# Gate matmuls of a recurrent unit on halves of the array's rows

## The chip, the cores and the metric

The kernel runs on one core of one Trainium2 chip. The metric is the device time of one launch in microseconds, as the median of several runs. The core's engines work side by side and wait for each other by semaphores: the matrix engine (PE, with its weight loads listed as PEld), the vector engine (DVE), the scalar engine (ACT), GpSimd (POOL), and SyncE (SP), which here issues most of the transfers.

## The reference

A decoder block: one wide input projection, dilated attention as one branch, a gated linear recurrence (RG-LRU) as the other, a merge, an output projection and a layer norm. There are 2048 positions of 1024 features. The change lies in the recurrence's gates, which are block-diagonal: 16 blocks of 64 features, each with a 64x64 matrix for either gate.

```python
def rg_lru(x, w_r, b_r, w_i, b_i, lam):
    xb = x.reshape(B, S, LRU_BLOCKS, LRU_BLOCK_WIDTH)      # 16 blocks of 64
    r = sigmoid(einsum('bsgi,gij->bsgj', xb, w_r).reshape(B, S, C) + b_r)
    i = sigmoid(einsum('bsgi,gij->bsgj', xb, w_i).reshape(B, S, C) + b_i)
    log_a = -LRU_C * r * softplus(-lam)
    a = exp(log_a)
    u = sqrt(maximum(-expm1(2.0 * log_a), 0.0)) * (i * x)
    # h_t = a_t h_{t-1} + u_t along the positions
```

## The kernel before

Everything is held with features on the 128 partitions and positions along the row, in four chunks (`c`, 0 to 3) of 512 positions. A feature tile has 128 features, so it holds two gate blocks. The numbers are float32; a product of two is made of three matmuls, high by high, high by low and low by high part, each part rounded to the engine's one-pass float32 (`F32R`).

The kernel has three stages, of which the first, up to about 1420 us, makes the input projection. Its loop (line 881) goes over `T` ticks: in each, `product` (line 597) issues 12 matmuls of 128x512 into one of four PSUM banks (`q`, line 614), then the events of that tick are issued (`prep_w`, line 268: rounding the next weights on ACT at line 274 and their low part on DVE or POOL), then `run_chains`, and then `evacuate`, by which DVE or ACT reads the bank. Half way through the 12 matmuls `run(pe_late)` (line 617) issues small PE work that was put off: transposes of values (`vtp`, line 366) and the gates of the recurrence (`g`, lines 482 to 484).

All else is done by generators, the chains. Each `yield Ask(...)` is a point where a chain goes on in a later tick: when enough ticks have passed (`lag`), enough of the 32 shared buffers are free (`need`, `keep`), its condition holds, and the tick's allowance of engine time (`LEN`, 2.75 us, less the estimates that `Ask` names) isn't used up. The estimates decide the order of the instructions on every engine; they are fixed numbers in the code.

`lru(i, c, ub)` (line 437) is the chain of feature tile `i` and chunk `c`: 8 tiles by 4 chunks are 32 of them. In order: at 16 of the 32 it brings both gates' weights to `gr` (lines 448 and 449, on SP's queue), already laid out on the host as 128x128 with two 64x64 blocks on the diagonal and zeros beside them. It makes the convolution `v`; splits the weights into `gw`, high and low part of either gate, four matrices of 128 columns (lines 466 and 467); splits `v` into `vh` and `vl`; and puts off `gates()` to the middle of the next tick's matmuls. `gates()` makes one bank for each gate, three matmuls each. Two ticks later ACT takes the tanh of either bank (lines 495 and 496; a sigmoid is made of a tanh), with the biases `brh`, then an exp and two more functions; DVE multiplies `ti` by `v` (line 500), and the rest ends in a scan (line 517). `gate["busy"]` keeps a second chain from issuing its gates before the tanh of the first are issued; the two banks of tag `g` are all that there are.

`lo_` and `up_` (line 301) are the partitions 0 to 63 and 64 to 127.

Of the kernel before, what the change touches and what calls it, by code (L numbers as in the profile page):

```python
# [8 lines left out]
F32 = mybir.dt.float32  # L9
F32R = mybir.dt.float32r  # L10
AF = mybir.ActivationFunctionType
ALU = mybir.AluOpType
# [3 lines left out]
P = 128  # L16
# [4 lines left out]
CH = 512  # L21
# [10 lines left out]
def hybrid_block_kernel(ctx: ExitStack, tc: tile.TileContext, a: dict, out: bass.AP):  # L32
    nc = tc.nc
    sp, act, dve, pool, pe = nc.sync, nc.scalar, nc.vector, nc.gpsimd, nc.tensor

    def flat(t):
        return t.bitcast(F32)
# [37 lines left out]
    brh = cst.tile([P, 2, 8], F32, name="brh")  # L75
# [33 lines left out]
    def pe_later(lag, fn):  # L109
        pe_late.append((now["n"] + lag, fn))  # L110
# [27 lines left out]
    ps = stA.enter_context(tc.tile_pool(name="ps", bufs=2, space=PSUM))  # L138
# [5 lines left out]
    def take(name, dt=F32R):  # L144
        if not vacant:
            raise RuntimeError(f"no slot at {now['n']}: {[x[1].name if hasattr(x[1],'name') else x[1] for x in home.values()]} chains {len(chains)}")
        i = vacant.pop(0)
        t = sl_p.tile([P, CH], dt, tag=f"s{i}", name=name)
        home[id(t)] = (i, t)
        return t  # L150

    def give(*ts):
        for t in ts:
            vacant.append(home.pop(id(t))[0])

    def give_sent(*ts):

        for t in ts:
            later(2, lambda t=t: give(t))
# [69 lines left out]
    def tt(eng, out, in0, in1, op):  # L229
        eng.tensor_tensor(out=out, in0=in0, in1=in1, op=op)  # L230
# [70 lines left out]
    lo_, up_ = slice(0, 64), slice(64, P)  # L301
# [129 lines left out]
    GLG, GW = {}, {}  # L431
# [5 lines left out]
    def lru(i, c, ub):  # L437
        nm = f"{i}_{c}"
        f = FT_U + i
        if c == 1 and i in put_off:  # L440
            yield Ask(lag=0, need=1, keep=1, cond=lambda: len(ub_free) > 1)
            ub = ub_free.pop(0)
            sp.dma_start(ub[:, 3:3 + CH], u_scr[i])
        bring_gw = c in ((0, 1) if i in put_off else (0, 2))
        if bring_gw:
            yield Ask(lag=0, need=1, keep=1)
            gr = take("gr" + nm, F32)
            sp.dma_start(gr[:, 0:P], a["wr"][i])
            sp.dma_start(gr[:, P:2 * P], a["wi"][i])
        if c == 1 and i in put_off:  # L450
            yield Ask(lag=4)
        yield Ask(lag=0, need=1, keep=6, cond=lambda: gate["live"] < 2 and begun[i] == c, ACT=1.3, DVE=2.7)
        gate["live"] += 1
        begun[i] += 1
        v = take("v" + nm, F32)
        act.activation(ub[:, 0:3], ubs[:, i, c, 0:3], AF.Copy)
        act.activation(v, ub[:, 0:CH], AF.Identity, scale=lrn[:, 0, i:i + 1], bias=lr[:, 4, i:i + 1])
        for j in range(1, 4):
            dve.scalar_tensor_tensor(out=v, in0=ub[:, j:j + CH], scalar=lrn[:, j, i:i + 1], in1=v,
                                     op0=ALU.mult, op1=ALU.add)  # L460
        act.activation(ubs[:, i, c + 1, 0:3], ub[:, CH:CH + 3], AF.Copy)
        ub_free.append(ub)
        if bring_gw:
            yield Ask(ACT=.4, DVE=.4, lag=2, need=1, keep=1)
            w = GW[i] = take("gw" + nm)
            act.activation(w[:, 0:2 * P], gr[:, 0:2 * P], AF.Copy)
            tt(dve, w[:, 2 * P:], gr[:, 0:2 * P], flat(w[:, 0:2 * P]), ALU.subtract)
            give(gr)
        yield Ask(lag=0, cond=lambda: gated[i] == c)
        gw = GW[i].rearrange("p (l j f) -> p l j f", l=2, j=2)  # L470
        yield Ask(need=2, keep=1, ACT=.66, DVE=.75)
        vh, vl = take("vh" + nm), take("vl" + nm)
        act.activation(vh, v, AF.Copy)
        tt(dve, vl, v, flat(vh), ALU.subtract)
        yield Ask(lag=2, cond=lambda: not gate["busy"])
        gate["busy"] = True
        pg = []

        def gates():
            for j in range(2):  # L480
                g = ps.tile([P, CH], F32, tag="g", name=f"g{j}{nm}", bufs=2)
                pe.matmul(g, gw[:, 0, j], vh, start=True, stop=False)
                pe.matmul(g, gw[:, 0, j], vl, start=False, stop=False)  # L483
                pe.matmul(g, gw[:, 1, j], vh, start=False, stop=True)
                pg.append(g)
            give(vh, vl)
            if c in ((0, 3) if i in put_off else (1, 3)):
                give(GW[i])

        pe_later(1, gates)  # L490
        gated[i] = c + 1
        yield Ask(lag=2, need=3, keep=1, ACT=3.3, DVE=.75)
        gate["busy"] = False
        tr, ti, e = take("tr" + nm, F32), take("ti" + nm, F32), take("e" + nm, F32)
        act.activation(tr, pg[0], AF.Tanh, scale=0.5, bias=brh[:, 0, i:i + 1])
        act.activation(ti, pg[1], AF.Tanh, scale=0.5, bias=brh[:, 1, i:i + 1])
        act.activation(e, tr, AF.Exp, scale=sp2n[:, i:i + 1], bias=sp2n[:, i:i + 1])
        act.activation(e, e, AF.Identity, scale=0.5, bias=half_t)
        act.activation(tr, tr, AF.Tanh, scale=sp2[:, i:i + 1], bias=sp2[:, i:i + 1])
        dve.scalar_tensor_tensor(out=ti, in0=ti, scalar=1.0, in1=v, op0=ALU.add, op1=ALU.mult)  # L500
        give(v)
        yield Ask(need=2, keep=1, ACT=2.0, DVE=2.2)
        s, w = take("sq" + nm, F32), take("nw" + nm, F32)
        act.activation(s, tr, AF.Sqrt)

        dve.scalar_tensor_tensor(out=w, in0=tr, scalar=1.0, in1=e, op0=ALU.add, op1=ALU.mult)
        dve.scalar_tensor_tensor(out=e, in0=w, scalar=2.0, in1=e, op0=ALU.subtract, op1=ALU.mult)
        dve.scalar_tensor_tensor(out=tr, in0=tr, scalar=2.0, in1=e, op0=ALU.mult, op1=ALU.mult)
        give(w)
        yield Ask(ACT=.66, DVE=1.5)  # L510
        act.activation(tr, tr, AF.Identity, bias=one_t)
        dve.scalar_tensor_tensor(out=s, in0=s, scalar=-1.0, in1=e, op0=ALU.mult, op1=ALU.mult)
        tt(dve, s, s, ti, ALU.mult)
        give(e, ti)
        yield Ask(need=1, keep=1, DVE=1.6, cond=lambda: done[i] == c)
        h = take("h" + nm, F32)
        dve.tensor_tensor_scan(out=h, data0=tr, data1=s, initial=hst[:, i, 0:1], op0=ALU.mult, op1=ALU.add)  # L517
        dve.tensor_copy(hst[:, i, 0:1], h[:, CH - 1:CH])
        done[i] = c + 1
        gate["live"] -= 1  # L520
        give(tr, s)
        if c == 1 and i in put_off:
            yield Ask(lag=0, need=1, keep=3)
            g = GLG[i, 1] = take("glg" + nm, F32)
            sp.dma_start(g, hb_scr[i * P:(i + 1) * P, CH:2 * CH])
            yield Ask(lag=2)
        yield Ask(POOL=1.4, cond=lambda: (i, c) in GLG)
        g = GLG.pop((i, c))
        tt(pool, g, g, h, ALU.mult)
        give(h)  # L530
        yield Ask()
        sp.dma_start(hb_scr[i * P:(i + 1) * P, c * CH:(c + 1) * CH], g)
        give_sent(g)
# [28 lines left out]
    def result(s, fi, c, bank, u):  # L562
# [10 lines left out]
        if kind in ("qk", "v"):  # L573
            y = take("y" + nm)
            total(flat(y), bank, u, f, sgn, True)
            start_chain(qk_chain(y, f, c) if kind == "qk" else v_chain(y, sgn, f, c))
        elif kind == "mg":
            y = take("y" + nm, F32)
            total(y, bank, u, f, sgn, False)
            start_chain(mg_chain(y, sgn, f, c))  # L580
        elif kind == "ga" or not fi:
            y = take("y" + nm, F32)
            total(y, bank, u, f, sgn, False)
            start_chain(silu_chain(y, sgn, f, c))
        else:
            i = f - FT_U
            if c == 1 and i in put_off:
                y = take("y" + nm, F32)
                total(y, bank, u, f, sgn, True)
                act.activation(ubs[:, i, 2, 0:3], y[:, CH - 3:CH], AF.Copy)  # L590
                start_chain(store_chain(y, u_scr[i]))
                return
            ub = ub_free.pop(0)
            total(ub[:, 3:3 + CH], bank, u, f, sgn, True)
            start_chain(lru(i, c, ub), 7 if c % 2 else 0)
# [92 lines left out]
    for s, pl in enumerate(plan):  # L688
        if pl[0] and pl[4] == "ug":
            i = pl[1][1][0] - FT_U  # L690
# [208 lines left out]
    n = len(where)  # L899
# [143 lines left out]
    for m in range(NB + 4):  # L1043
        u, n = divmod(m, 16)
# [167 lines left out]
    for n in range(32):  # L1212
        c, f = divmod(n, 8)
# [200 lines left out]
```

## Time and profile before

| what | us |
|---|---|
| median of 3 runs | 2268.6 |
| runs | 2268.6, 2264.68, 4475.0 |
| the profiled execution's own time | 2267.38 |
| its span in the profile | 2265.6 |
| mean granted PE clock in it | 0.992 |

A row of a table of instructions names the line of the kernel, the engine, the operation, what is written and read, how many there are, their busy time in us and the mean of one in ns, and after the second bar the engine's idle time before them with what ended it. A row of waits has who waited for whom, the us in total, how many times, and the longest. A row of the timeline has the start, the time taken, the engine and the instruction; neighbours that are alike are merged and counted. Ends of matmuls are modelled, so starts are what can be compared. In a table by stretches each row has the stretch, its length, and the busy us and instructions of PE, PEld, DVE, ACT and POOL, then the granted PE clock as a share, and the transfers' share and GB/s.

### The profile page before, as it was taken

What the parts mean: (1) busy time and instruction counts of PE and PEld (TensorE: products, weight loads), DVE (VectorE), ACT (ScalarE), POOL (GpSimd) and SP (SyncE); (2) the same over time, 40 slices, a digit from 0 to 9 for tenths busy, and PEclk for the clock granted to TensorE, in tenths of its full rate; (3) what the DMA queues carried; (4) which work ended last, traced back from release to release, by engine and by line L of the source; (5) the groups of instructions that cost most, each with busy time, mean ns of one, the idle gap of its engine ahead of it and who ended that gap; (6) DMA issues with size and microseconds to landing.
All of it is one profiled execution on the core that took longest, in us unless ns stands there. A gap on an engine that the chain in (4) does not pass through costs nothing.

```text
span 2265.6 us, 33610 instructions
## 1 busy us (share of the span) xinstructions
PE 2212.9 (98%) x11032; PEld 1867.7 (82%) x11032; DVE 1755.2 (77%) x3246; ACT 1209.0 (53%) x2161; POOL 819.4 (36%) x604
## 2 busy tenths in 40 slices
PE   8999999999999999999999999989999999989998
PEld 6888888888887888888888888879999888868886
DVE  7888898899888786877878877646666578856676
ACT  5456566666565566766677776546666511121100
POOL 1555455455543011201201200466776255521220
PEclk9999999999999999999999999999999999989999
DMA  6977977977977666666665756886986588763431
GB/s 211 258 232 221 266 235 234 253 230 246 263 239 254 218 186 204 218 176 201 217 204 189 236 176 209 248 233 159 257 209 158 170 290 280 247 196 135 158 121 66
DMA packets 305055, 481.64 MB, mean 213 GB/s; under 512 B 90177, under 2 KB 131169, under 8 KB 300273
## 3 DMA queue, kind: packets, MB, share of 16 engines
q1 hardware_dynamic: 275888, 437.61, 62.2%
q0 software_dynamic: 9888, 17.90, 5.0%
q10 hardware_dynamic: 19104, 23.99, 3.4%
q8 instruction: 88, 1.44, 0.3%
q14 instruction: 87, 0.70, 0.1%
HBM read 303.17 MB, written 176.23 MB: 212 GB/s over the span
## 4 chain that ended last, share of the span: by engine, by line
PE 76%; DMA 8%; issue 5%; DVE 5%; POOL 3%; ACT 2%; SPq 1%; ACTq 0%; DVEq 0%; POOLq 0%
PE q L614 58%; PE o L988 3%; PE s L949 2%; DMA A<-qh_scr 2%; PE pt L964 1%; PE z L1294 1%; PE z L1293 1%; PE z L1292 1%; POOL C L797 1%; PE yb L1184 1%; DMA gB<-mg_scr 1%; PE yb L1182 1%; PE yb L1183 1%; PE vtp L366 1%; POOL me L1263 1%
## 5 line engine op out<-in xcount | busy, mean ns | idle before, releaser
L614 PE MATMUL q<-xT,hS 128*128 128x512 f32 x1632 | 504.0, 390 | 1.4 <-DVE y L230 1.4
L614 PE MATMUL q<-xB,hA 128*128 128x512 f32 x1344 | 417.8, 392 | 8.7 <-ACT xB L218 8.0
L614 PE MATMUL q<-xT,l 128*128 128x512 f32 x1088 | 423.6, 389 | 0.0
L614 PE MATMUL q<-xB,l 128*128 128x512 f32 x944 | 368.6, 391 | 0.0
L614 PEld LDWEIGHTS q<-xT,hS 128*128 128x128 f32 x1632 | 305.3, 188 | 64.7 <-issue 1.8
L614 PEld LDWEIGHTS q<-xB,hA 128*128 128x128 f32 x1344 | 252.6, 189 | 62.1 <-ACT xB L218 8.0
L614 PEld LDWEIGHTS q<-xT,l 128*128 128x128 f32 x1088 | 204.2, 188 | 42.7
L955 ACT ACTIVATE p<-p,osb 128x256 f32<-128x256 f32 (+1 forms) x384 | 156.3, 454 | 114.7 <-DVE osb L953 110.4
L614 PEld LDWEIGHTS q<-xB,l 128*128 128x128 f32 x944 | 177.8, 188 | 37.3
L953 DVE CUSTOM_DVE_ANT_0 p<-s,mask 128x256 f32<-128x256 f32 (+1 forms) x384 | 125.3, 364 | 100.0 <-PE s L949 64.7
L230 POOL TENSOR_TENSOR sw<-sw,sin 128x512 f32<-128x512 f32 x96 | 154.3, 1630 | 122.6 <-ACT sw L318 111.8
L230 POOL TENSOR_TENSOR y<-y,h 128x512 f32<-128x512 f32 x28 | 40.3, 1438 | 414.4 <-DVE h L517 338.1
L988 PE MATMUL o<-V,ptb 128*128 128x65 f32 x1200 | 165.0, 276 | 11.1 <-ACT ptb L969 8.5
L988 PEld LDWEIGHTS o<-V,ptb 128*128 128x128 f32 x1200 | 151.8, 195 | 22.9 <-ACT ptb L969 19.9
L614 PE MATMUL q<-xB,hS 128*128 128x512 f32 x544 | 168.6, 391 | 0.3 <-DVE v L230 0.3
L614 PE MATMUL q<-xT,hA 128*128 128x512 f32 x544 | 168.2, 390 | 0.1
L274 ACT ACTIVATE hA<-wA 128x512 fp32r<-128x512 f32 x220 | 138.7, 635 | 21.2 <-PE g L483 6.6
L274 ACT ACTIVATE hS<-S 128x512 fp32r<-128x512 f32 x170 | 108.5, 638 | 62.8 <-DVE S L230 55.6
L230 POOL TENSOR_TENSOR l<-wA,hA 128x512 fp32r<-128x512 f32 x68 | 108.5, 1595 | 83.0 <-ACT hA L274 64.3
L949 PE MATMUL s<-B,A 128*128 128x256 f32 (+1 forms) x384 | 115.8, 323 | 6.3 <-POOL B L795 4.4
L614 PEld LDWEIGHTS q<-xT,hA 128*128 128x128 f32 x544 | 101.6, 188 | 21.4 <-issue 0.6
L614 PEld LDWEIGHTS q<-xB,hS 128*128 128x128 f32 x544 | 101.3, 188 | 21.3 <-issue 0.7
(199 smaller groups left out, 4922.3 us busy)
## 6 DMA issues: line engine op xcount, KB each, us to landing
wA<-in_w_in_dram SPq DMA_DIRECT2D x219, 256.0 KB, 4.5
wl_scr<-l SPq DMA_DIRECT2D x102, 512.0 KB, 4.7
l<-wl_scr SPq DMA_DIRECT2D x102, 512.0 KB, 4.0
wS<-in_w_in_dram SPq DMA_DIRECT2D x102, 256.0 KB, 3.9
wS<-in_w_in_dram POOLq DMA_DIRECT2D x68, 256.0 KB, 7.0
mg_scr<-y SPq DMA_DIRECT2D x59, 256.0 KB, 5.0
o_scr<-osb ACTq DMA_DIRECT2D x48, 264.0 KB, 6.0
oc<-o_scr SPq DMA_DIRECT2D x48, 264.0 KB, 5.0
```

The source lines that it names most:

```text
L230: eng.tensor_tensor(out=out, in0=in0, in1=in1, op=op)
L274: act.activation(heads(h), heads(r, False), AF.Copy)
L366: pe.transpose(tp[:, b, :], flat(vt)[:, b * P:(b + 1) * P], ident)
L614: pe.matmul(bank, w[:, ks], x[:, kk, xx], start=(first and i == 0), stop=(last and i == 11))
L797: eng.tensor_tensor(out=b2[hs, h, t], in0=flat(b2[hs, h, t]), in1=flat(B1[hs, h, t]), op=ALU.subtract)
L949: pe.matmul(s[:, h, (0 if g == 2 and n else lo):256], q, k, start=(i == 0), stop=(i == 1))
L953: dve.tensor_tensor_reduce(out=p[:, h, lo:256], in0=s[:, h, lo:256], in1=mask[:, lo:256], scale=1.0, scalar=3e38, op0=ALU.add, op1=ALU.min ...
L955: act.activation(p[:, h, lo:256], p[:, h, lo:256], AF.Exp, scale=-1.0, bias=mm)
L964: pe.transpose(pt[:, 2 * h + x, :], p[:, h, x * P:(x + 1) * P], ident)
L988: pe.matmul(o[:, n % 2, h * 65:h * 65 + 65], ptb[:, 2 * h + x, :], V[:, kb, vo + h * 65:vo + h * 65 + 65], start=(x == lo // P), stop=(x = ...
L1182: pe.matmul(yb, WL[f][:, 0, k], xx[:, 0], start=(k == 0), stop=False)
L1183: pe.matmul(yb, WL[f][:, 0, k], xx[:, 1], start=False, stop=False)
```

## The change

The weights of a feature tile come without the zeros: of each gate's 128x128 only the two 64x64 blocks on the diagonal are loaded, each to its own half of the partitions, the first gate's to columns 0 to 63 and the second's to 64 to 127. So the rounding and subtraction work on 128 columns instead of 256. A matmul of `gates()` now takes 64 partitions of weights and of `v`, a block of 64 features, and makes both gates of that block at once: 64 rows of output for `r`, 64 for `i`. The lower block goes to one bank, the upper to the other, and the two alternate. Six matmuls of 512 columns stay six of 512 columns.

In a bank the rows now are a block's two gates, and no longer one gate's 128 features. Four tanh, each over 64 partitions, put them back: `r` of both blocks to `tr`, `i` of both to `ti`, so that all that follows is as before. The estimates in the `Ask` lines stay what they were.

```diff
@@ lru(i, c, ub)
-            sp.dma_start(gr[:, 0:P], a["wr"][i])
-            sp.dma_start(gr[:, P:2 * P], a["wi"][i])
+            for j, n in enumerate(("wr", "wi")):
+                for hs in (lo_, up_):
+                    sp.dma_start(gr[hs, 64 * j:64 * j + 64], a[n][i][hs, hs])
...
-            act.activation(w[:, 0:2 * P], gr[:, 0:2 * P], AF.Copy)
-            tt(dve, w[:, 2 * P:], gr[:, 0:2 * P], flat(w[:, 0:2 * P]), ALU.subtract)
+            act.activation(w[:, 0:P], gr[:, 0:P], AF.Copy)
+            tt(dve, w[:, P:2 * P], gr[:, 0:P], flat(w[:, 0:P]), ALU.subtract)
...
-        gw = GW[i].rearrange("p (l j f) -> p l j f", l=2, j=2)
+        gw = GW[i].rearrange("p (l f) -> p l f", f=P)
...
-            for j in range(2):
-                g = ps.tile([P, CH], F32, tag="g", name=f"g{j}{nm}", bufs=2)
-                pe.matmul(g, gw[:, 0, j], vh, start=True, stop=False)
-                pe.matmul(g, gw[:, 0, j], vl, start=False, stop=False)
-                pe.matmul(g, gw[:, 1, j], vh, start=False, stop=True)
-                pg.append(g)
+            pg.extend(ps.tile([P, CH], F32, tag="g", name=f"g{j}{nm}", bufs=2) for j in range(2))
+            for n, (l, x) in enumerate(((0, vh), (0, vl), (1, vh))):
+                for g, hs in zip(pg, (lo_, up_)):
+                    pe.matmul(g, gw[hs, l], x[hs], start=(n == 0), stop=(n == 2))
...
-        act.activation(tr, pg[0], AF.Tanh, scale=0.5, bias=brh[:, 0, i:i + 1])
-        act.activation(ti, pg[1], AF.Tanh, scale=0.5, bias=brh[:, 1, i:i + 1])
+        for j, (t, fr) in enumerate(((tr, lo_), (ti, up_))):
+            for g, hs in zip(pg, (lo_, up_)):
+                act.activation(t[hs], g[fr], AF.Tanh, scale=0.5, bias=brh[hs, j, i:i + 1])
```

What stands in a row on PE at the first of the 32 sets, before. A row has the line, the operation, what it writes and reads by name (the numbers after a name tell instances apart), and the shape written; `gw` are the gate weights, `vh` and `vl` the two parts of the convolution's result.

```order
L366 MATMUL vtp_0_1220<-ident,y_0_1164 128x128 x4
L482 MATMUL g_0_1225<-vh_0_1160,gw_0_1133 128x512
L483 MATMUL g_0_1225<-vl_0_1161,gw_0_1133 128x512
L484 MATMUL g_0_1225<-vh_0_1160,gw_0_1133 128x512
L482 MATMUL g_0_1229<-vh_0_1160,gw_0_1133 128x512
L483 MATMUL g_0_1229<-vl_0_1161,gw_0_1133 128x512
L484 MATMUL g_0_1229<-vh_0_1160,gw_0_1133 128x512
L614 MATMUL q_5_1213<-xB_259,hA_5_1128 128x512 x2
```

The banks came one after the other, three matmuls each. The same place in the changed kernel, where line 484 is the one call of matmul in `gates()`:

```order
L366 MATMUL vtp_0_1222<-ident,y_0_1166 128x128 x4
L484 MATMUL g_0_1227<-vh_0_1162,gw_0_1135 128x512
L484 MATMUL g_0_1228<-vh_0_1162,gw_0_1135 128x512
L484 MATMUL g_0_1227<-vl_0_1163,gw_0_1135 128x512
L484 MATMUL g_0_1228<-vl_0_1163,gw_0_1135 128x512
L484 MATMUL g_0_1227<-vh_0_1162,gw_0_1135 128x512
L484 MATMUL g_0_1228<-vh_0_1162,gw_0_1135 128x512
L614 MATMUL q_5_1215<-xB_259,hA_5_1130 128x512 x2
```

Now the banks alternate; what stands ahead of the set and behind it has not moved, and that holds for all 32 sets. On ACT, the tanh of the same set before, between the weights' rounding (`hA`, line 274) and the functions that follow:

```order
L274 ACTIVATE hA_5_1263<-wA_5_1053 128x4x2x64
L495 ACTIVATE tr_0_1267<-g_0_1225,brh 128x512
L496 ACTIVATE ti_0_1268<-g_0_1229,brh 128x512
L497 ACTIVATE e_0_1269<-tr_0_1267,sp2n 128x512
L498 ACTIVATE e_0_1269<-e_0_1269,half_t 128x512
```

The same place after the change, where line 496 is the one call of the four tanh:

```order
L274 ACTIVATE hA_5_1265<-wA_5_1055 128x4x2x64
L496 ACTIVATE tr_0_1269<-g_0_1227,brh 64x512
L496 ACTIVATE tr_0_1269<-g_0_1228,brh 64x512
L496 ACTIVATE ti_0_1270<-g_0_1227,brh 64x512
L496 ACTIVATE ti_0_1270<-g_0_1228,brh 64x512
L497 ACTIVATE e_0_1271<-tr_0_1269,sp2n 128x512
L498 ACTIVATE e_0_1271<-e_0_1271,half_t 128x512
```

Two instructions became four, each on half of the partitions; DVE's, POOL's and SP's order is as before, but for the four loads in the place of two at 16 places.

## The prediction

> **What bounds the kernel now.** I read the page first, then the chain of waits, the table by stretches, the matrix engine's (PE's) waits, and last the timeline around one set of gate matmuls.
>
> ```profile
> span 2265.6 us, 33610 instructions
> PE 2212.9 (98%) x11032; PEld 1867.7 (82%) x11032; DVE 1755.2 (77%) x3246; ACT 1209.0 (53%) x2161; POOL 819.4 (36%) x604
> PE 76%; DMA 8%; issue 5%; DVE 5%; POOL 3%; ACT 2%; SPq 1%; ACTq 0%; DVEq 0%; POOLq 0%
> ```
>
> PE is busy 98% of the span and carries 76% of the chain. The change lies in the first stage, which runs to about 1420 us; the gate matmuls stand between 114 and 1403 us. The chain in that window, and the same time by stretches (each column is an engine's busy us, then its instructions):
>
> ```profile
> by line: PE q L614 89.8%; PE vtp L366 1.6%; PE g L484 1.1%; PE g L482 1.1%; PE g L483 1.1%; issue 1.0%; DVE S L230 0.8%; DVE y L230 0.5%; DVE u L230 0.2%; DVE rp L230 0.2%; DVE v L230 0.2%; DVE h L517 0.2%; DVE l L230 0.2%; ACT hA L274 0.1%
> 114.00:500.00 386.00, 386.00 (x1747) 319.51 (x1746) 342.56 (x405) 230.58 (x382) 198.63 (x149) 1.00 0.82 238
> 500.00:720.00 220.00, 218.06 (x959) 179.24 (x958) 199.70 (x235) 135.84 (x217) 115.95 (x86) 1.00 0.80 243
> 720.00:1403.00 683.00, 682.41 (x3056) 564.73 (x3055) 545.72 (x778) 466.57 (x759) 90.04 (x64) 1.00 0.67 207
> PE q L614 <- DVE y L230: 1.4, 1, 1.4
> PE q L614 <- DVE u L230: 0.6, 1, 0.6
> PE q L614 <- DVE v L230: 0.3, 1, 0.3
> ```
>
> The reader is to see that PE has no hole here: the last three rows are all its waits for other engines between 60 and 1410 us, 2.3 us together. So a microsecond of PE work taken out is a microsecond off the span, as long as the others keep up. The three gate lines are 3.3% of the 1289 us window, about 43 us; that is all the matmul time there is to touch. DVE is 199.70 of 220 us busy in the middle stretch (91%), and it empties PE's banks: there is the least room. ACT is at 60 to 68% (230.58 of 386, 466.57 of 683).
>
> PE's price is the distance between starts, not the duration. One set of gates, matmuls and then weight loads:
>
> ```profile
> 495.84 0.39 PE L614 MATMUL q<-xB,l 128*128 128x512 f32 x1
> 496.06 0.39 PE L482 MATMUL g<-vh,gw 128*128 128x512 f32 x1
> 496.29 0.39 PE L483 MATMUL g<-vl,gw 128*128 128x512 f32 x1
> 497.20 0.39 PE L484 MATMUL g<-vh,gw 128*128 128x512 f32 x1
> 497.42 0.39 PE L614 MATMUL q<-xB,hA 128*128 128x512 f32 x1
> ...
> 496.07 0.19 PEld L483 LDWEIGHTS g<-vl,gw 128*128 128x128 f32 x1
> 496.29 0.19 PEld L484 LDWEIGHTS g<-vh,gw 128*128 128x128 f32 x1
> ```
>
> Six matmuls from 496.06 to 497.42: 1.36 us, 0.227 us each, though one lasts 0.39 us; the remaining 0.16 us is its tail, hidden by the next. The 0.19 us weight load starts with the matmul before its own and is hidden too.
>
> **The change, part by part.** *Gate matmuls.* Six of 128 rows by 512 columns become six of 64 rows by 512 columns. Their count and their columns stay, so one alone costs 0.227 us as before. The gain exists only if a lower-half and an upper-half matmul run at the same time. The trace has no such pair: a pair costs between 0.227 (fully together) and 0.454 us (one after the other). I take 0.227, since two distinct halves with two weight sets and two banks share nothing visible, and since PE can issue fast enough:
>
> ```profile
> 113.66 0.60 PE L366 MATMUL vtp<-ident,y 128*128 128x128 f32 x4
> 114.02 0.48 PE L482 MATMUL g<-vh,gw 128*128 128x512 f32 x1
> 114.33 0.40 PE L483 MATMUL g<-vl,gw 128*128 128x512 f32 x1
> ```
>
> Four weight loads with their four transposes take 0.36 us (113.66 to 114.02), 0.09 each; two in 0.18 us fit under 0.227. Three pairs are 0.68 us, where six stood at 1.36: 0.68 us saved in a set, at 32 sets 21.8 us.
>
> *The switch.* Each set goes from matmuls on all 128 rows to halves and back. No row shows a change of row tiling. Nearest in kind is the step from transposes to gates above: 0.31 us from 114.02 to 114.33 instead of 0.227, so 0.08 us. The upper end is the hidden tail and the hidden weight load both laid bare: 0.16 + 0.19 = 0.35 us. The lower end is zero. I take the tail alone, 0.16 us, because a switch that separates two ways of using the same array should let the last matmul out but need not hold back the loading. Twice a set that is 0.32 us, 32 times 10.2 us; the ends are 0 and 22.4 us.
> The Trainium skill speaks against the change here: "TensorEngine Tiling (Array Packing)", Key Properties, says that a change of the tiling mode, not of the tile alone, drains the engine. No run here shows it yet and the page gives no figure; by the 0.08 us of the row the net would be about 16.7 us, by a drain read as the tail it is the 11.6 us of my sum.
>
> So a set goes from 1.36 to 1.00 us, 0.36 saved; 32 sets: 11.6 us.
>
> *Tangents.* Two tanh over 128 partitions become four over 64. ACT's rows with either height:
>
> ```profile
> L496 ACT ACTIVATE ti<-g,brh 128x512 f32<-128x512 f32 x32 | 21.9, 683 | 0.0
> L274 ACT ACTIVATE hS<-wS 128x512 fp32r<-128x512 f32 x102 | 64.8, 637 | 12.4 <-DVE y L407 5.2 <-POOL l L230 2.4 <-DVE h L517 1.7
> L317 ACT ACTIVATE sw<-y 64x512 f32<-64x512 f32 x96 | 60.6, 631 | 66.8 <-DVE y L558 59.7 <-issue 5.2 <-POOL l L230 0.4
> 502.28 0.67 ACT L495 ACTIVATE tr<-g,brh 128x512 f32<-128x512 f32 x1
> 502.84 0.69 ACT L496 ACTIVATE ti<-g,brh 128x512 f32<-128x512 f32 x1
> 503.41 0.81 ACT L497 ACTIVATE e<-tr,sp2n 128x512 f32<-128x512 f32 x1
> 505.58 0.39 PE L482 MATMUL g<-vh,gw 128*128 128x512 f32 x1
> ```
>
> A copy of 64 partitions takes 631 ns, one of 128 takes 637: half the height saves nothing. So two more tanh, one every 0.56 us (502.28, 502.84, 503.41): 1.13 us a set, 36 us more ACT work. ACT has the room on average. Behind the tanh on ACT stand the exp, the next weights' rounding (L274) and the bank copies; behind them waits DVE at L500, and behind DVE the banks. The closest successor set starts at 505.58, 2.1 us after the tanh that read the same banks end (502.84 + 0.69), so 0.9 us remain and PE should not wait for the banks of the gates either. What is late next is DVE:
>
> ```profile
> DVE ti L500 <- ACT ti L496: 23.5, 14, 5.6
> 520.00:560.00 40.00, 40.00 (x179) 33.11 (x178) 39.38 (x45) 25.36 (x39) 25.94 (x19) 1.00 0.78 248
> 680.00:720.00 40.00, 38.16 (x167) 30.66 (x166) 37.61 (x41) 20.78 (x33) 19.86 (x15) 1.00 0.66 210
> ```
>
> DVE waits for that tanh in 14 of 32 sets already, and around 540 and 700 us it is 94 to 98% full. If each of the 14 costs 1.13 us more and all of it reached PE, that were 15.8 us; the other end is 0. The cover is DVE's free time (137 us between 720 and 1403), and it is thin only for the sets between about 500 and 720 us. For those I take a loss of 2 us in all, near the lower end, since PE's whole waiting in the stage is 2.3 us now.
>
> *Weights.* Two loads of 128x128 become four of 64x64, with half the bytes, and the rounding and subtraction go from 256 to 128 columns:
>
> ```profile
> L448 SPq DMA_DIRECT2D gr<-in_wr_dram x16: 328/383/831, 91.9 to 1363.4; - x16
> L449 SPq DMA_DIRECT2D gr<-in_wi_dram x16: 422/465/1593, 92.4 to 1363.8; - x16
> L466 ACT ACTIVATE gw<-gr 128x256 fp32r<-128x256 f32 x16 | 6.4, 402 | 1.0 <-DMA gr<-in_wi_dram 0.8
> SPq L296 <- PE q L614: 197.7, 73, 6.4
> ```
>
> SP issues two more in 16 places, at 0.38 to 0.47 us each 0.9 us a place, some 14 us in all. They stand ahead of the next weights' loads on SP's queue, which itself waits 197.7 us for free buffers at one line alone; those waits are the cover, and without them the next weights would come 0.9 us late at 16 places. The first reader, at L466, waited 0.8 us for its load in all sets together. I cost this at 0. The smaller rounding saves ACT and DVE at most 0.2 us each at 16 places, off the path: 0.
>
> **The sum.** 21.8 - 10.2 - 2 = 9.6 us off the profiled execution, which took 2267.4 us as a run (2265.6 of span and 1.8 around it): 2258 us. The median of the runs is 2268.6, 1.2 above that execution; the forecast is 0.4 to 0.5% under either. A difference within 2% is about what a measurement of this kernel can't tell from no change.
>
> **The rivals.** *The halves take turns.* If the second half's matmul waits for the first, six still cost 1.36 us and the switches come on top: 32 x 0.32 = 10.2, plus the 2 us, 2280 us; with switches of 0.08 it is 2275. This is the case of the other side: it decides as soon as a pair costs more than 0.35 us (three pairs and 0.32 make 1.36). For it speaks that each matmul streams 512 columns through one engine and that the trace has never two at once; against it, that the halves need nothing of each other.
> *A free switch.* The array takes up halves without a gap: 21.8 us less 2, 2248 us. For it speaks that weight loads already run beside matmuls, so only the tail is in question; against it, the 0.08 us row.
> *Weights of a half wait for its own matmul.* Then a pair costs 0.227 + 0.19 = 0.42 us, a set 1.57, 0.21 more than now, and 2276 us. The rows from 496.07 speak against it, where a load starts beside the matmul that uses the same rows. By the Trainium skill ("TensorE: Matmul & The Clock Gate", Part 3, what overlaps) a weight load overlaps matmuls in flight only when its row group differs; these rows disagree, so it gets a small chance.
> *ACT's longer chain reaches PE.* At the upper end of its term all 15.8 us come through: 2267.4 - 11.6 + 15.8 = 2272 us; it decides from 11.6 us on, where the gain is gone. For it speaks DVE's 98% around 540 us; against it, 2.3 us of waits in 1350 us.
> *Every change of half counts as a switch.* Six times 0.39 + 0.19 are 3.5 us, 2.1 more a set: 2335 us. Nothing here speaks for it.
>
> **How the numbers follow.** Forecast (pairs together, a switch of about a tail): 0.52, its own range 2250 to 2265. Free switch 0.15; halves in turn 0.16; waiting weights 0.05; ACT's chain 0.09; every change a switch 0.03. From 2246 (the free switch at its best) to 2278 lie the forecast, the free switch and most of the others: what is left out above is part of the halves in turn and the last rival, about 0.13. Faster by over 2% would need 45 us, more than all gate matmuls last: 0.01. Slower by over 2% is the last rival: 0.03. The rest, 0.96, lies within 2%.
>
> **What would show it.** In the profile after, the six starts of a set should come in three near-equal pairs, 0.23 us from pair to pair, with gaps of 0.1 to 0.2 us at the first and the one after the last; the next q matmul then starts 1.0 us after the first gate instead of 1.36. Starts every 0.227 us show the halves in turn. ACT's busy time rises by about 43 us (64 tanh of 0.68), and PE's waits for DVE stay under 5 us to 1410 us; more than that is ACT's chain. A stage that ends about 10 us sooner, with the later stages as long as before, is the forecast. It is wrong if pairs don't overlap, or if a switch costs over twice the tail.

## The result and the profile after

| | before | after |
|---|---|---|
| median of 5 runs, us | 2268.6 | 2276.32 |
| ratio of the runs | 1 | 1.0052 (95% interval 1.004 to 1.0065) |
| span of the profiled execution, us | 2265.6 | 2274.3 |

The ratio leaves out one slow launch of the kernel before, which took 4475 us, and is not the quotient of the two medians; against the 2264.8 to 2265.2 us that the kernel before took beside the experiments below, 2276.32 us is 1.005.

The change makes the kernel half a per cent slower, where 0.4 to 0.5% faster was forecast and 2278 was the end of the range. The measured difference lies within 2%, but its interval is clear of 1: the prediction took 2% for about what a measurement of this kernel can't tell from no change, and the intervals here are 0.2 to 0.4% wide.

The head of the page after, and the row of its chain of waits by engine:

```profile
span 2274.3 us, 33751 instructions
PE 2213.1 (97%) x11032; PEld 1846.6 (81%) x11032; DVE 1753.8 (77%) x3246; ACT 1257.1 (55%) x2225; POOL 818.4 (36%) x604
PE 57%; DVE 5%; issue 5%; DMA 5%; ACT 4%; POOL 2%; SPq 0%; ACTq 0%; DVEq 0%; POOLq 0%
```

ACT's busy time rose by 48 us (1209.0 to 1257.1), for two more tangents in 32 sets. PE's busy time is the same. The chain's 57% for PE can't be set beside the 76% of before: the shares of this row add up to 78%, because the chain was followed back only to about 492 us, and before it reached the start. Over 500 to 1400 us, which both chains cover, the matmuls of `q` make up 87.8% of it before and 79.4% after: there something else stands ahead of PE more often.

The matmuls did what the change says. The timeline of PE and of its weight loads after, around the set whose rows of before were shown:

```profile
497.21 0.39 PE L614 MATMUL q<-xB,l 128*128 128x512 f32 x1
497.53 0.50 PE L484 MATMUL g<-vh,gw 64*128 64x512 f32 x2
497.87 0.40 PE L484 MATMUL g<-vl,gw 64*128 64x512 f32 x2
498.10 0.40 PE L484 MATMUL g<-vh,gw 64*128 64x512 f32 x2
498.43 0.73 PE L614 MATMUL q<-xB,hA 128*128 128x512 f32 x2
499.00 0.39 PE L614 MATMUL q<-xB,l 128*128 128x512 f32 x1
...
497.53 0.19 PEld L484 LDWEIGHTS g<-vh,gw 64*128 64x128 f32 x2 [0.35 <-issue]
498.43 0.30 PEld L614 LDWEIGHTS q<-xB,hA 128*128 128x128 f32 x2 [0.37 <-issue]
```

The form reads 64*128, and each row is two matmuls that together last about as long as one (0.50, 0.40 and 0.40 us): they run at the same time. From the q matmul ahead to the set are 0.32 us where 0.23 is usual, from the first pair to the second 0.34, to the third 0.23, to the next q matmul 0.33, and that one and its successor take 0.57 instead of 0.45 (498.43 to 499.00). These gaps are some 0.42 us in a set. From 497.21 to 499.00 are 1.79 us; before, the same nine steps of 0.227 were 2.04. A set thus gains 0.25 us, and 32 sets 8 us.

PE's waits for other engines after, between 60 and 1410 us, and DVE's longest one for ACT:

```profile
PE q L614 <- DVE u L230: 7.5, 6, 3.3
PE q L614 <- DVE y L230: 3.2, 1, 3.2
PE q L614 <- DVE y L558: 2.9, 3, 1.2
PE q L614 <- DVE v L230: 1.2, 3, 0.5
PE vtp L366 <- DVE y L558: 0.9, 4, 0.3
...
DVE ti L500 <- ACT ti L496: 53.7, 21, 6.8
```

PE's waits are 15.7 us, 2.3 before, and all are for DVE, which is to empty a bank. DVE's wait for the tangent of the input gate went from 23.5 us in 14 places to 53.7 in 21.

How much later the same matmul starts after than before, found by matching PE's q matmuls in their order:

| at, us of before | later by, us | what lies ahead of it |
|---|---|---|
| 345 | -0.9 | six sets, three short waits (0.2 to 0.3 us) |
| 552 | 4.9 | five stalls between 464 and 541 of the run after, three sets |
| 702 | 8.2 | more stalls, the longest of them (3.2 us) near the end; three sets |
| 1014 | 6.1 | eight sets, no stall to speak of |
| 1046 | 10.8 | one stall of 2.8 us and slow matmuls |
| 1177 | 9.6 | five sets |
| 1209 | 14.7 | one stall of 3.3 us and slow matmuls |
| 1402 | 12.9 | seven sets |

Where nothing stalls, each set gains its 0.25 us (2.1 in eight sets to 1014, 1.8 in seven to 1402); a few stalls take back more than all 32 sets bring. The last q matmul starts at 1463.4 us before and at 1476.3 after, and the span ends 8.7 us later. The 4 us between are no effect of the change: in the fifteen profiles of this document the time from the last q matmul to the end lies between 797 and 807 us, though no edit touches these stages. (The first stage thus ends near 1463 us, not near 1420 as the text ahead has it; the gates' window ends at 1403 all the same.)

### The profile page after: what moved, and what is told of

Its sections match the earlier page's. It is cut to its first block, busy times and chain, and to the rows that moved or that the text cites. A ratio compares the mean times of both kernels' runs of the same rounds, so it can differ in the third digit from the quotient of the medians.

```text
span 2274.3 us, 33751 instructions
## 1 busy us (share of the span) xinstructions
PE 2213.1 (97%) x11032; PEld 1846.6 (81%) x11032; DVE 1753.8 (77%) x3246; ACT 1257.1 (55%) x2225; POOL 818.4 (36%) x604
## 4 chain that ended last, share of the span: by engine, by line
PE 57%; DVE 5%; issue 5%; DMA 5%; ACT 4%; POOL 2%; SPq 0%; ACTq 0%; DVEq 0%; POOLq 0%
PE q L614 34%; PE o L988 4%; PE s L949 3%; PE yb L1184 2%; PE yb L1182 2%; PE yb L1183 2%; PE pt L964 2%; PE z L1294 1%; PE z L1292 1%; PE z L1293 1%; DMA A<-qh_scr 1%; POOL me L1263 1%; PE g L484 1%; DVE S L230 1%; ACT p L955 1%
## 5 line engine op out<-in xcount | busy, mean ns | idle before, releaser
L274 ACT ACTIVATE hA<-wA 128x512 fp32r<-128x512 f32 x220 | 138.6, 635 | 12.7 <-PE g L484 4.3
```

Source lines behind the costliest of these rows:

```text
L274: act.activation(heads(h), heads(r, False), AF.Copy)
```

## The experiments

Every run was made in five rounds beside the kernel before on the same chip, whose medians there were 2264.8 to 2265.2 us. The ratio is to these.

### Tangents alone, pairs alone, the loads, the estimate

The first four take the change apart. In the kernel before, only the tangents are cut:

```diff
-        act.activation(tr, pg[0], AF.Tanh, scale=0.5, bias=brh[:, 0, i:i + 1])
-        act.activation(ti, pg[1], AF.Tanh, scale=0.5, bias=brh[:, 1, i:i + 1])
+        for j, (t, g) in enumerate(zip((tr, ti), pg)):
+            for hs in (lo_, up_):
+                act.activation(t[hs], g[hs], AF.Tanh, scale=0.5, bias=brh[hs, j, i:i + 1])
```

> The kernel before with only its two tangents cut into four of 64 partitions, each in its own rows of its own bank; matmuls and loads as before. If ACT's longer chain (through DVE's wait at the first product with the tangent, then the banks) is what cost the gain: slower than before by 15 to 22 us, 2284 to 2291, with PE's waits in the first stage at 15 to 25 us instead of 2.3. If DVE has no room for a faster PE in any case: within 4 us of before, because PE is not faster here. If the two more loads on SP's queue cost it: no change.

Measured: 2282.64 us, ratio 1.0079 (1.0065 to 1.0094), 17.9 us slower. PE's waits in the first stage are 13.4 us, all for DVE, with the longest near 1052 and 1220 us where the changed kernel has them:

```profile
PE q L615 <- DVE u L230: 6.6, 4, 3.4
PE q L615 <- DVE y L559: 3.0, 3, 1.2
PE q L615 <- DVE y L230: 2.1, 1, 2.1
PE vtp L366 <- DVE y L559: 1.4, 3, 0.9
PE q L615 <- DVE v L230: 0.3, 1, 0.3
```

Both are a little under what was expected of ACT's longer chain (2284 to 2291 us, and waits of 15 to 25). The matmuls are those of before, so four tangents in the place of two cost 18 us with no crossing of halves and no faster PE.

In the changed kernel, only the tangents are those of before:

```diff
-        for j, (t, fr) in enumerate(((tr, lo_), (ti, up_))):
-            for g, hs in zip(pg, (lo_, up_)):
-                act.activation(t[hs], g[fr], AF.Tanh, scale=0.5, bias=brh[hs, j, i:i + 1])
+        act.activation(tr, pg[0], AF.Tanh, scale=0.5, bias=brh[:, 0, i:i + 1])
+        act.activation(ti, pg[1], AF.Tanh, scale=0.5, bias=brh[:, 1, i:i + 1])
```

> The changed kernel with two tangents of 128 partitions as before the change, so that the halves are not put back and the gates of the two blocks are mixed; pairs of matmuls and the four small loads as in the change. If ACT's longer chain cost the gain: faster than before by 9 to 12 us, 2256 to 2260, PE's waits 2 to 5 us. If DVE has no room for a faster PE: 2264 to 2272, the saved 0.37 us a set coming back as PE's waits for DVE. If the loads cost it: 2272 to 2278.

Measured: 2257.94 us, ratio 0.9965 (0.9951 to 0.9978), 6.9 us faster; PE's waits are 2.2 us:

```profile
PE q L613 <- DVE u L230: 1.8, 2, 1.0
PE q L613 <- DVE v L230: 0.4, 1, 0.4
```

The pairs are worth 7 us (5 to 11 by the interval), where 9 to 12 were expected, counting 0.37 us a set; the gaps at the switches leave 0.25. DVE has the room for a faster PE; the theory that it has none falls. The two parts add up to the whole: 17.9 - 6.9 = 11, and the change is 0.5% (9 to 15 us) slower. The profiles show it closer still, by the start of the last q matmul: 20.6 us later than before with the tangents alone, 8.0 earlier with the pairs alone, 12.9 later with the change.

The loads, with weights that lie side by side in memory:

```diff
-            for j, n in enumerate(("wr", "wi")):
-                for hs in (lo_, up_):
-                    sp.dma_start(gr[hs, 64 * j:64 * j + 64], a[n][i][hs, hs])
+            sp.dma_start(gr[:, 0:64], a["wr"][i])
+            sp.dma_start(gr[:, 64:P], a["wi"][i])
```

> The changed kernel with the gates' weights stored side by side in memory, so that each place has two loads of 128x64 instead of four of 64x64. If SP's two more issues cost the gain: 2258 to 2268. If ACT's longer chain or DVE's lack of room did: 2274 to 2279, as the change.

Measured: 2280.95 us, ratio 1.007 (1.0055 to 1.0084), 2 us above the number expected if ACT or DVE is the cause, and not faster than the change. The two more loads are not the cause.

The planner's estimate for the tick of the tangents:

```diff
-        yield Ask(lag=2, need=3, keep=1, ACT=3.3, DVE=.75)
+        yield Ask(lag=2, need=3, keep=1, ACT=4.5, DVE=.75)
```

> The changed kernel with one number changed: the planner's estimate of ACT's time in the tick of the tangents, 4.5 instead of 3.3, so that it puts less other work for ACT into those ticks. If ACT's longer chain is the cause and can be planned around: 2262 to 2271, PE's waits under 10 us. If DVE has no room, or the loads are the cause: 2274 to 2280, as the change.

Measured: 2277.59 us, ratio 1.0055 (1.0036 to 1.0074). PE's waits for DVE fell, others for ACT came in their place, 12.7 us in all: telling the planner of the time moves the stalls and removes none of the loss.

### The product with the input gate

DVE stands at line 500 until the tangent is there, with the bank copies queued behind it. My theory after the first four was that this one wait is the way. Three runs tested it. The product a tick later, in the changed kernel and, as a control, in the kernel before:

```diff
-        dve.scalar_tensor_tensor(out=ti, in0=ti, scalar=1.0, in1=v, op0=ALU.add, op1=ALU.mult)
-        give(v)
         yield Ask(need=2, keep=1, ACT=2.0, DVE=2.2)
+        dve.scalar_tensor_tensor(out=ti, in0=ti, scalar=1.0, in1=v, op0=ALU.add, op1=ALU.mult)
+        give(v)
```

> The changed kernel with DVE's product of the input gate with v moved behind the next point of the planner, at least one tick later, so that DVE does not stand at it while ACT works through the four tangents. If DVE's wait at that product is the way by which ACT's longer chain reaches the banks: PE's waits in the first stage fall from 16 us to under 8 and the time is 2258 to 2268. If ACT's greater load hurts by its other work (weights rounded late, banks copied late), whatever DVE does: 2273 to 2280.

> The kernel before with the same product a tick later and nothing else, as the control to the run on the changed kernel. If the product's place only matters where ACT is late: within 3 us of before. If it is worth something by itself, that is taken off what the run on the changed kernel shows; at most 4 us faster, since PE's waits here are 2.3 us.

The tangents of the input gate ahead of the others:

```diff
-        for j, (t, fr) in enumerate(((tr, lo_), (ti, up_))):
+        for j, (t, fr) in ((1, (ti, up_)), (0, (tr, lo_))):
```

> The changed kernel with the two tangents of the input gate ahead of those of the other gate: the same work for ACT, but what DVE waits for first is ready after two of the four. If DVE's wait at that product is the way: its wait falls from 54 us towards the 24 of before, and the time is 2258 to 2270. If ACT's load as such is: 2273 to 2280.

Measured: 2284.88 us (1.0088, 1.0074 to 1.0102), 2272.47 (1.0035, 1.0021 to 1.0049) and 2283.69 (1.0078, 1.0063 to 1.0093). The theory falls, though two of the times also lie above the 2273 to 2280 of the other one. DVE's wait did shrink as meant, to 27.2 us with the input gate first and to 5.1 with the product later, but it came back at the next places where DVE needs ACT. The waits of DVE with the input gate first:

```profile
DVE ti L500 <- ACT ti L496: 27.2, 17, 5.5
...
DVE tr L508 <- ACT sq L504: 16.2, 15, 2.0
...
DVE nw L506 <- ACT tr L499: 12.9, 10, 2.4
```

In the changed kernel the last two were 11.7 and 2.1 us, and before 9.2 and 1.6. The control missed both of its numbers and shows something more: in the kernel before, a shift of one instruction by a tick costs 0.35% by itself, 8 us. That is also the step from the changed kernel (1.0052) to the same with the product later (1.0088), so with the control taken off the move neither helps nor hurts. The order is tight enough that a small move of DVE's work reaches PE, whose waits in the first stage are 5.8 us in the control.

### Taking ACT's time out elsewhere, and putting it in alone

If ACT's time in the set is the cause, whoever waits for it, then less of other ACT work must help, and the same time without any use must hurt. The first leaves out two of ACT's instructions behind the tangents:

```diff
-        act.activation(e, e, AF.Identity, scale=0.5, bias=half_t)
...
-        act.activation(tr, tr, AF.Identity, bias=one_t)
```

> The changed kernel without two of ACT's other instructions of each set, the halving of the exp and the addition of one behind it (the decays are then wrong); pairs, four tangents and loads as in the change. This takes 1.2 to 1.3 us of ACT's work out of a set, where the tangents put 1.65 in. If ACT's time in the set is what reaches the banks, through several waits of DVE and not one: 2256 to 2263, PE's waits for DVE under 6 us. If cutting the tangents by partitions costs in another way than by ACT's time: 2268 to 2280.

Measured: 2270.19 us, ratio 1.0018 (1.0006 to 1.003), PE's waits 10.2 us. It helps by about a third of a per cent, more than half of the loss against before, and not by all of it. The time lies in the range of the other theory (2268 to 2280, near its fast end), and PE's waits are over the 6 us of the first: by itself this run speaks for neither.

One of the two on POOL, in the changed kernel and in the kernel before:

```diff
-        act.activation(tr, tr, AF.Identity, bias=one_t)
+        pool.tensor_scalar(out=tr, in0=tr, scalar1=1.0, scalar2=None, op0=ALU.add)
```

> The changed kernel with the addition of one (an instruction of ACT behind the tangents) made on POOL instead. It takes 0.6 us a set from ACT. If ACT's time in the set is the cause: about a third of the 18 us comes back, 2266 to 2273, unless POOL's instruction holds up DVE, which reads the same memory. If not: 2274 to 2284.

> The kernel before with the addition of one on POOL, the control: PE waits only 2.3 us there, so ACT's time saved is worth at most 2 us; within 4 us of before, and slower only if POOL holds up DVE.

Measured: 2278.57 us (1.0055, 1.0037 to 1.0072) and 2264.03 (0.9992, 0.9982 to 1.0002). In the kernel before it does nothing, as expected; in the changed one it does not help, against the expectation of a third. DVE is not held up by POOL there, as far as waits show it: it waits 4.5 us for POOL in the first stage, and 5.0 in the changed kernel.

The step behind the tangents two ticks later instead of one (`lag=2` in its `Ask`):

> The changed kernel with the step behind the tangents (root, and three of DVE's products) at least two ticks later instead of one; the product with the input gate stays where it is. If DVE is held by several waits for ACT, one after another, and this one is among them: 2266 to 2274. If only ACT's total matters, or the product with the input gate: 2274 to 2284.

Measured: 2277.1 us, ratio 1.0047 (1.0031 to 1.0064). That is the range for ACT's total, or the product, as the cause, but the stalls moved: those near 700, 1050 and 1210 us are gone in its trace and others stand between 170 and 400 us.

Now the same time without the cut. Pairs with two whole tangents, as in the run of the pairs alone, and two tangents of 64 partitions into a buffer that is written over:

```diff
+        act.activation(e[lo_], pg[0][lo_], AF.Tanh)
         act.activation(tr, pg[0], AF.Tanh, scale=0.5, bias=brh[:, 0, i:i + 1])
+        act.activation(e[up_], pg[1][up_], AF.Tanh)
         act.activation(ti, pg[1], AF.Tanh, scale=0.5, bias=brh[:, 1, i:i + 1])
```

> Pairs with two tangents of 128 partitions (the halves not put back), and between them two more tangents of 64 partitions whose result nobody uses. Nothing that follows needs more than before; only ACT is busy for 1.3 to 1.65 us longer ahead of the input gate's tangent. If ACT's time at this place is the whole cost: 2273 to 2281, like the change, with DVE's wait at the product with the input gate at 45 to 60 us and PE's waits at 12 to 18. If the cost lay in cutting the results by partitions or in the crossing of halves: 2256 to 2264, like the pairs alone.

Measured: 2277.95 us, ratio 1.0056 (1.0044 to 1.0068), against 0.9965 for the pairs alone. Time, DVE's wait and PE's waits (12.4 us) all lie where they were expected if ACT's time is the cost. Its waits are close to those of the change (line 501 is the former 500):

```profile
PE q L615 <- DVE u L230: 6.3, 5, 3.2
PE q L615 <- DVE y L230: 3.2, 1, 3.2
PE q L615 <- DVE y L559: 2.0, 3, 1.1
...
DVE ti L501 <- ACT ti L497: 49.2, 21, 6.5
```

From the first tangent to the exp are 2.39 us in the median of its 32 sets, 1.16 without the two idle tangents and 2.81 in the changed kernel. So 1.23 us of ACT's time at this place cost 20 us of the whole, here spent on tangents whose result nobody uses. ACT's time at this place is thus the cause, through whichever wait of DVE it comes, and not the crossing of halves.

The last run put the two half measures together: two ACT instructions less, and the product a tick later.

> The changed kernel without the two other instructions of ACT, as in the run that gave back half, and with the product with the input gate a tick later, so that DVE does not stand at it. If the half that stayed is DVE's wait at that product: 2256 to 2264. If moving the product costs as much as it did on the kernel before (some 8 us): 2268 to 2280.

Measured: 2274.37 us, ratio 1.0042 (1.0029 to 1.0056), slower than with two less alone. The time lies in the range of the second number; moving the product cost 4 us here, where it cost 8 in the kernel before.

## Why the prediction was wrong, point by point

**What bounds the kernel, and the gate matmuls: right.** The halves run together, a pair every 0.23 us after the first, and 0.68 us of matmul time in a set are saved.

**The switch: right in kind, small in size.** I took 0.16 us twice, 0.32 a set; the gaps are 0.42, 0.21 for a switch, since each shows twice: 0.1 us at its first matmul and 0.1 again behind that. A set saves 0.25 us where 0.36 was forecast, and 32 sets 8 us where the sum had 11.6. By "TensorEngine Tiling (Array Packing)" of the Trainium skill, Key Properties, a change of the tiling mode drains the engine; the trace agrees as far as it goes, since the weight load behind the switch starts 0.35 us after the end of the last one, together with its own matmul and no longer with the one ahead (497.53 us), near the modelled end of that one (497.60). The rivals of halves in turn, of waiting weights, of a free switch and of a switch at every half fall with the same rows, and the 0.08 us row was too low a guide.

**The tangents: this step failed, twice.** Its price was 1.13 us of ACT a set, from tangents that start every 0.56 us. ACT's timeline at the same place before and after:

```profile
1186.71 0.69 ACT L495 ACTIVATE tr<-g,brh 128x512 f32<-128x512 f32 x1
1187.30 0.68 ACT L496 ACTIVATE ti<-g,brh 128x512 f32<-128x512 f32 x1
1187.87 0.81 ACT L497 ACTIVATE e<-tr,sp2n 128x512 f32<-128x512 f32 x1
```

```profile
1198.20 1.38 ACT L496 ACTIVATE tr<-g,brh 64x512 f32<-64x512 f32 x2
1199.60 1.38 ACT L496 ACTIVATE ti<-g,brh 64x512 f32<-64x512 f32 x2
1201.00 0.82 ACT L497 ACTIVATE e<-tr,sp2n 128x512 f32<-128x512 f32 x1
```

Two of full height took 1.16 us to the exp, four of half height 2.80: 0.70 each, not 0.56. The set is 1.64 us longer on ACT. The profile of before could have told: the half-height copies of lines 317 and 318, of which the prediction read the 631 ns, follow each other at 0.64 us from start to start in all 96 pairs, without the overlap of 0.1 us that the whole tangents have.

The larger error is what reaches PE. I took 2 us, with DVE's free time as the cover, and cited 137 us of it between 720 and 1403. The run with the tangents alone shows 18 us. DVE's free time is no cover, because at this place it consists of waiting for ACT: DVE and ACT take turns in a fixed order, and what ACT is later by goes on to DVE. Over all sets DVE's wait for the tangent rose by 30.2 of the 52 us that ACT has more to do there. DVE's timeline, before and then after:

```profile
1188.02 0.69 DVE L500 SCALAR_TENSOR_TENSOR ti<-ti,v 128x512 f32<-128x512 f32 x1 [2.52 <-ACT ti L496]
```

```profile
1201.01 0.69 DVE L500 SCALAR_TENSOR_TENSOR ti<-ti,v 128x512 f32<-128x512 f32 x1 [4.03 <-ACT ti L496]
1214.18 3.35 DVE L230 TENSOR_TENSOR S<-S,wA 128x512 f32<-128x512 f32 x2
1217.46 0.68 DVE L230 TENSOR_TENSOR wS<-wS,wA 128x512 f32<-128x512 f32 x1
1218.06 0.74 DVE L558 SCALAR_TENSOR_TENSOR ub<-q,bn,v 128x512 f32<-128x512 f32 x1
1218.72 0.67 DVE L230 TENSOR_TENSOR u<-u,q 128x512 f32<-128x512 f32 x1
```

Matched instruction by instruction, DVE and ACT are 10.07 us later than before ahead of the set at 1166 us (of before), 11.49 behind its tangents, and 13.13 behind the next set's, while PE is only 9.6 later: two sets ten microseconds apart have put the pair of engines 3.5 us further behind PE. They keep that lag until PE needs a bank. The four q banks cover it until DVE reaches its long sums at 1214 us, a place where PE waited 0.6 us for DVE already before. Then PE stands, and is 13.1 us later behind the stall, as DVE is:

```profile
1215.81 0.39 PE L614 MATMUL q<-xB,l 128*128 128x512 f32 x1
...
1219.54 0.70 PE L614 MATMUL q<-xB,hA 128*128 128x512 f32 x2 [3.34 <-DVE u L230]
```

The rival "ACT's longer chain reaches PE" was thus the right one, with 0.09 and with 2272 us at its upper end; its price was bounded by the 14 sets in which DVE already waited, and DVE came to wait in 21. Its sign came true as well: PE's waits for DVE are 15.7 us, where over 5 was to be ACT's chain. That two other rivals had 2275 and 2276 us, the measured time, is chance: their mechanisms are not in the rows.

**A part that the prediction did not have: the clock.** After the two longest stalls in this half of the stage PE runs slowly for some microseconds. The stretches around the stall above (the granted clock stands behind POOL's count):

```profile
1205.00:1216.00 11.00, 10.54 (x47) 8.21 (x45) 10.08 (x12) 7.42 (x14) 5.38 (x4) 1.00 0.30 99
1216.00:1219.50 3.50, 0.20 (x1) 0.00 (x0) 3.50 (x5) 1.80 (x2) 0.98 (x1) 1.00 1.00 279
1219.50:1224.00 4.50, 4.46 (x13) 3.56 (x14) 4.50 (x7) 2.64 (x5) 0.00 (x0) 0.62 0.54 205
1224.00:1230.00 6.00, 6.00 (x28) 4.99 (x27) 5.29 (x8) 5.62 (x12) 0.00 (x0) 1.00 0.80 248
```

The granted clock is 0.62 for 4.5 us behind a stall of 3.34, and the matmuls there start up to 0.43 us apart. By late starts, matched as in the table, this adds 1.6 us (13.1 to 14.7), and as much behind the stall near 1051 us: 3 us of the 21 that the stalls and their wake take from the stage (13 late, and 8 saved). "TensorE: Matmul & The Clock Gate" of the Trainium skill, What's actually happening, has the clock halved after an idle window of about 3.4 us that runs freely, whenever the idle time begins. The trace agrees on the half: within the 4.5 us the granted clock is 0.50 for 3.4 us, from 1220.4 us on. It does not agree on the window, and there the measurement decides: the stalls that were followed by the half clock are shorter, 3.34 and 2.82 us here and one of 1.91 us near 1049 us in the run with idle tangents, while the one of 3.17 us that ended at 710.26 us left the clock at 1.00. So in these runs a stall of 2 to 3 us sometimes cost another 1.6 behind it, and sometimes did not.

**The loads: right** at nothing, by the run with two loads. The smaller rounding was put at nothing too; no run has it alone.

**The later stages: right.** I had them as long as before; the 4 us between the two profiles lie within what single executions differ by.

What stays open: why taking 1.2 us out of ACT behind the tangents gave back only part, and why moving one product in the kernel before costs 0.35%. Both say that the stalls depend on where DVE's and ACT's instructions fall in each of a few places, not on their sum alone; no run here predicts which. And nothing tried beats the kernel before with a whole computation: the one run that is faster, by 0.35%, leaves the halves where they are.

## What to carry to other kernels

Idle time of an engine covers nothing if it is spent in waiting, in a fixed order, for the very engine that is to get more work; ask then how far the two may fall behind the bound engine before it needs them, here the banks covered 3.5 us for some 18 us, and none of it at the next place where DVE was slow. Price a cut in height on ACT at its full rate from starts, and for the form that it will have: half the partitions gave no discount, and with the halves in turn the overlap of neighbours was lost. A saving on the bound engine of 0.25 us a set was worth that only where nothing stalled; run the cost side alone and the gain side alone before judging the sum.

## What the runs showed of the hardware that was not expected

Tangents over 64 partitions, the halves in turn, start 0.70 us apart, those over 128 partitions 0.57 us apart; the cost is there without any crossing of halves (0.70 in the run of the tangents alone). The height is not what loses the overlap. In the run with idle tangents whole ones stand between a lower half (line 494) and an upper (line 496):

```profile
116.99 0.57 ACT L494 ACTIVATE e<-g 64x512 f32<-64x512 f32 x1
117.46 0.68 ACT L495 ACTIVATE tr<-g,brh 128x512 f32<-128x512 f32 x1
118.15 0.59 ACT L496 ACTIVATE e<-g 64x512 f32<-64x512 f32 x1
118.77 0.69 ACT L497 ACTIVATE ti<-g,brh 128x512 f32<-128x512 f32 x1
119.36 0.80 ACT L498 ACTIVATE e<-tr,sp2n 128x512 f32<-128x512 f32 x1
```

The whole tangent behind the lower half starts 0.10 us before that ends, as the exp does behind a whole tangent. Into the upper half and out of it nothing overlaps, and the medians of the 32 sets say the same. In the changed kernel, too, the first tangent of a set, on the lower half, starts 0.11 us before the end of a rounding, in the 15 sets where one stands directly ahead. So the overlap is lost next to an instruction that reads or writes the upper half alone. Whether it would be lost between two on the same half no run shows, since none has them in a row.

DVE's sums take 1.67 us each near 1214 us instead of 0.69 while POOL multiplies beside them, from 1211.86 us for 5.12 (two sums in 3.35, above). They did so in the kernel before at the same place, so this is no part of the difference; that the lag comes due there because of it is likely, and not shown by a run.
